# The second block's mixer laid out anew: recurrence projected first, attention scores by pairs of heads, and the feed-forward's first weight splits earlier

## The chip, the core and the metric

The kernel runs on one core of a Trainium2 chip. The metric is device time in microseconds (us). The engines are TensorE (PE in the rows; PEld is its weight load), VectorE (DVE), ScalarE (ACT), GpSimd (POOL) and SyncE (SP, which here only issues DMA transfers). A trailing q, as in SPq, stands for an engine's queue.

## What is computed

Two transformer blocks on 256 tokens of width 1024 in fp32. The first holds two attention mixers and a mixture of 32 experts, and its weights of some 400 MB fill most of the time. The change lies in the second block, which is, cut to what matters:

```python
h = rms_norm(x, g_pre_mix)
q, k, v, xr, gr = split(h @ w_in)                     # 5 chunks of 512 columns
attn = softmax(q k^T / 8 + bias, causal) @ v          # 8 heads of 64
xr = causal_dwconv(xr, w_conv_lru, b_conv_lru)        # 4 taps
r = sigmoid(xr @ w_r + b_r); i = sigmoid(xr @ w_i + b_i)   # block-diagonal
log_a = -8 * r * softplus(-lam); a = exp(log_a)
u = sqrt(-expm1(2 * log_a)) * (i * xr)
lru = scan(h_t = a_t * h_(t-1) + u_t) * gelu(gr)
x = x + rms_norm(concat([attn, lru]) @ w_out, g_post_mix)
h = rms_norm(x, g_pre_ffn)
up = causal_dwconv(h @ w_up)                          # 2 * 2816 columns, 3 taps
x = x + rms_norm((gelu(up_g) * up_u) @ w_down, g_post_ffn)
```

## The kernel before, in words

**Precision.** Each weight and each activation is split into a high part rounded to fp32r (a copy on ScalarE, tiles `wh`, `uh`, `mxh`) and a low part, the rest (a subtraction on VectorE, tiles `wl`, `ul`, `mxl`). A product is three matmuls, high by high, high by low and low by high (`mm3`, L288 to L291). `split` (L267) and `row_split` (L1280) do this for a tile of 128 x 1024 of a weight. They take their tiles from the pool `ws`, which in the second block has 5 buffers of each name (L1291).

**Order.** The code lists instructions in program order. A planner inside the framework then lays out the queue of each engine: it lets an engine take the earliest instruction of the program that it holds to be ready, by its own costs. On the chip each queue runs in the order so fixed. `tc.issue_after` adds an edge to this plan. PSUM has 8 banks in this part, 4 named `acc` (`acc_tile`) and 4 named `wk` (`work_tile`), each name a ring.

**Weights.** The list `plan` (L182 to L217) gives the order in which SyncE loads them, each into one of 3 ring buffers (`NRING_A`, L90). `done(key)` frees a buffer once its last split has read it, and that issues the next load of the list. For the second block the list is: 5 chunks of `w_in` ("in2": v, q, k, xr, gr), 2 halves of `w_out` ("o2"), then 11 chunks of `w_up` with 6 of `w_down` between them.

**The stages around the change.**

- `x2_norm` (L1408) makes the first block's final norm and the second block's first one: sums of squares on ScalarE, `rsq` and `rs_sum` with a power on GpSimd, and `spread_tile` (L338), which turns the column `r2` into a row `rB` by a matmul. `rB` scales every projected chunk when it leaves PSUM.
- The projection loop (before the line `for _ in heads`, L1600) runs 16 weight tiles of 24 matmuls, 4 a chunk in the order q, k, xr, gr (`seq`). `presplit(j + 2)` stands ahead of the matmuls of tile j. After xr come `conv` (L1455); after gr come `lru_gates` (L1461, block-diagonal matmuls and tanh) and `lru_a` (L1468, exp, tanh, square).
- From the third chunk on, two steps of the generator `attention` (L1547) follow each tile. `a_s(h)` (L1498) makes one head's scores (contraction over 64 rows) and its softmax, `a_t(h)` (L1520) transposes them, `a_o(p)` (L1529) multiplies by v for two heads. It uses an `acc` bank.
- Behind the loop `lru_b` (L1482) has square root, gelu and scan, and `mxh`/`mxl` 4 to 7 (the recurrence's half of the input of `w_out`) are split.
- `nat2` (L1310) runs `w_out`: 48 matmuls of 512 columns with the first half (rows of the attention), whose four row tiles are split ahead as `first`, then 48 with the second. `epi2` (L1648) holds the norms behind it; while the second 128 tokens go through theirs, 24 dummy matmuls run.
- `split_up(i)` (L1615) splits the feed-forward's weight tile i. Tiles 0 to 2 are split ahead of `nat2`; the low parts of 0 and 1 are made on GpSimd (`eng=G`), that of 2 on VectorE. Tile 1 borrows the buffers `xc`, `ig`, tile 2 `rg`, `vN`. Tile 3 comes behind the transposes at the end of `epi2`.

Of the kernel before, what the change touches and what calls it, by code (L numbers as in the profile page):

```python
# [25 lines left out]
FT = mybir.dt.float32  # L26
FR = mybir.dt.float32r
# [77 lines left out]
def block_kernel(ctx: ExitStack, tc: tile.TileContext, A, out, dbg=None, parts=("t1", "moe", "over", "t3")):  # L105
# [105 lines left out]
    for c in range(2):  # L211
        want(("o2", c), wo2[c], [P, 4, 1024])
# [541 lines left out]
    ts(ch, ch, -4.0, None, OP.mult)  # L754

# [652 lines left out]
    def x2_norm(t):  # L1408
        rms_halves(r1[:, t:t + 1], xn[:, t], sm)
        tt(xn[:, t], xn[:, t], gfin, OP.mult)  # L1410
        ss = sm.tile([P, 1], FT, name="ss", bufs=4)
        sumsq(ss, xn[:, t], tp.tile([P, D], FT, name="junk2"))
        ts(ss, ss, r1[:, t:t + 1], r1[:, t:t + 1], OP.mult, OP.mult)
        rsq(r2[:, t:t + 1], ss, D, sm)
        tt(r2[:, t:t + 1], r2[:, t:t + 1], r1[:, t:t + 1], OP.mult)
        ts(xn[:, t], xn[:, t], r1[:, t:t + 1], None, OP.mult)
# [51 lines left out]
    def lru_a(hf):  # L1468
# [5 lines left out]
        for m in (2 * hf, 2 * hf + 1):  # L1474
            act(a_[:, m], rg[:, m], AF.Exp, scale=ch[:, m:m + 1], bias=ch[:, m:m + 1])
            ts(rg[:, m], rg[:, m], ch[:, m:m + 1], ch[:, m:m + 1], OP.mult, OP.add)
        stt(ig[:, ms], ig[:, ms], 1.0, xc[:, ms], OP.add, OP.mult)
        act(rg[:, ms], rg[:, ms], AF.Tanh, scale=-1.0)
# [19 lines left out]
    def a_s(h):  # L1498
        z = work_tile()
        p, r0 = h // 2, 64 * (h % 2)  # L1500
        PE.matmul(z[:, 0:P], qT[r0:r0 + 64, p, 0:P], kT[r0:r0 + 64, p, 0:P], start=True, stop=False,
                  skip_group_check=True)
        PE.matmul(z[:, P:384], qT[r0:r0 + 64, p, P:S], kT[r0:r0 + 64, p, 0:S], start=False, stop=True,
                  skip_group_check=True)
        s = mx_.tile([P, 384], FT, name="as", bufs=3)
        tt(s[:, 0:P], z[:, 0:P], Bt[:, h, P:S], OP.add)
        tt(s[:, P:384], z[:, P:384], Bt[:, h], OP.add)
        nm = sm.tile([P, 2], FT, name="nm", bufs=4)
        V.reduce_max(nm[:, 0:1], s[:, 0:P], axis=AX, negate=True)
        V.reduce_max(nm[:, 1:2], s[:, P:384], axis=AX, negate=True)  # L1510
        rs = sm.tile([P, 2], FT, name="rsum", bufs=4)
        act(s[:, 0:P], s[:, 0:P], AF.Exp, bias=nm[:, 0:1], accum_out=rs[:, 0:1])
        act(s[:, P:384], s[:, P:384], AF.Exp, bias=nm[:, 1:2], accum_out=rs[:, 1:2])
        rc = sm.tile([P, 2], FT, name="rcp", bufs=4)
        V.reciprocal(rc, rs)
        ts(s[:, 0:P], s[:, 0:P], rc[:, 0:1], None, OP.mult)
        ts(s[:, P:384], s[:, P:384], rc[:, 1:2], None, OP.mult)
        pm[h] = s
# [10 lines left out]
    def a_o(p):  # L1529
        o = acc_tile()  # L1530
# [16 lines left out]
    def attention():  # L1547
        a_s(0)
        yield
        for h in range(8):  # L1550
            if h + 1 < 8:
                a_s(h + 1)
                yield
            a_t(h)
            if h % 2 == 1:
                a_o(h // 2)
            yield
# [14 lines left out]

    heads = attention()
    presplit(0)
    presplit(1)
    for j, ((i, hf, m), _) in enumerate(seq):
# [6 lines left out]
        if m == 1:  # L1583
            if i == 1:
                stt(qT[:, sl], ps, 0.125, rB2, OP.mult, OP.mult)
            elif i == 2:
                tt(kT[:, sl], ps, rB2, OP.mult)
            elif i == 3:
# [3 lines left out]
            else:  # L1592
# [70 lines left out]
    for i in range(3):  # L1663
        split_up(i)
# [186 lines left out]
```

## Time and profile before

| what | value |
|---|---|
| median of 3 runs (lowest to highest) | 1423.74 us (1421.06 to 1424.24) |
| the profiled execution, its time | 1422.5 us |
| its span, first to last instruction | 1420.5 us |
| TensorE matmul busy | 1315.2 us (93%) |
| VectorE busy | 627.6 us (44%) |
| ScalarE busy | 371.8 us (26%) |
| GpSimd busy | 40.0 us (3%) |
| mean DMA rate | 340 GB/s |

The time is the span and some 2 us around it. Busy shares are means over stages with different limits: the experts fill the middle of the span with DMA at 427 GB/s, the second block runs from about 1081 us to the end. Matmuls are pipelined, so their recorded durations overlap; what one of a stream costs is the distance between the starts of neighbours. The idle time in brackets at the end of a timeline row is that of the engine just before the row's instruction, with the engine that ended it.

### The profile page before, as it was taken

What the parts mean: (1) busy time and instruction counts of PE and PEld (TensorE: products, weight loads), DVE (VectorE), ACT (ScalarE), POOL (GpSimd) and SP (SyncE); (2) the same over time, 40 slices, a digit from 0 to 9 for tenths busy, and PEclk for the clock granted to TensorE, in tenths of its full rate; (3) what the DMA queues carried; (4) which work ended last, traced back from release to release, by engine and by line L of the source; (5) the groups of instructions that cost most, each with busy time, mean ns of one, the idle gap of its engine ahead of it and who ended that gap; (6) DMA issues with size and microseconds to landing.
All of it is one profiled execution on the core that took longest, in us unless ns stands there. A gap on an engine that the chain in (4) does not pass through costs nothing.

```text
span 1420.5 us, 19855 instructions
## 1 busy us (share of the span) xinstructions
PE 1315.2 (93%) x8393; PEld 744.0 (52%) x8394; DVE 627.6 (44%) x1250; ACT 371.8 (26%) x641; POOL 40.0 (3%) x54
## 2 busy tenths in 40 slices
PE   8989999999998888889998888988888998999997
PEld 7777543434333333333343333333335886899997
DVE  6766532332322232222232222322226878677776
ACT  5654211101100010001110001100014658555554
POOL 1010200000000000000000000000000101000000
PEclk9999999999999999999999999999999999999999
DMA  7366899999999999999999999999998523355530
GB/s 287 112 239 270 340 427 427 426 427 426 427 427 427 427 427 426 425 412 427 427 427 427 427 428 427 427 426 427 427 426 350 188 103 134 138 196 197 196 149 31
DMA packets 40591, 482.40 MB, mean 340 GB/s; under 512 B 4104, under 2 KB 4640, under 8 KB 12592
## 3 DMA queue, kind: packets, MB, share of 16 engines
q1 hardware_dynamic: 39232, 477.99, 81.2%
q0 software_dynamic: 832, 2.62, 0.6%
q8 instruction: 68, 1.11, 0.3%
q10 hardware_dynamic: 432, 0.46, 0.1%
q14 instruction: 27, 0.22, 0.0%
HBM read 479.99 MB, written 1.06 MB: 339 GB/s over the span
## 4 chain that ended last, share of the span: by engine, by line
DMA 47%; PE 45%; DVE 4%; issue 2%; ACT 2%; POOL 1%; DVEq 0%; ACTq 0%; SPq 0%; POOLq 0%
DMA w<-w_gu 25%; DMA w<-w_dn 19%; PE gu L1086 10%; PE y L1122 4%; PE acc L289 3%; PE acc L290 3%; PE acc L291 3%; PE wk L290 3%; PE wk L291 3%; PE wk L289 3%; DMA w<-w_pg 2%; PE pj L289 1%; PE pj L291 1%; PE pj L290 1%; PE xg L1056 1%
## 5 line engine op out<-in xcount | busy, mean ns | idle before, releaser
L1086 PE MATMUL gu<-w,xg 128*64 128x512 f32 x2048 | 470.1, 601 | 45.2 <-DMA w<-w_gu 39.1
L1086 PEld LDWEIGHTS gu<-w,xg 128*64 128x64 f32 x2048 | 141.6, 137 | 315.4 <-issue 249.8
L1122 PE MATMUL y<-w,gl 128*64 128x512 f32 x1024 | 233.1, 597 | 28.9 <-DMA w<-w_dn 27.2
L121 ACT ACTIVATE h<-gu,gs 128x512 f32<-128x512 f32 x64 | 40.5, 683 | 558.8 <-PE gu L1086 558.8
L124 DVE TENSOR_TENSOR h<-sc,h 128x512 f32<-128x512 f32 x126 | 81.4, 686 | 201.0 <-PE sc L1146 198.5
L273 DVE TENSOR_TENSOR wl<-w,wh 128x1024 fp32r<-128x1024 f32 (+2 forms) x124 | 147.5, 1200 | 45.5 <-ACT wh L121 45.0
L1122 PEld LDWEIGHTS y<-w,gl 128*64 128x64 f32 x1024 | 73.5, 136 | 161.3 <-issue 157.9
L121 ACT ACTIVATE wh<-w 128x1024 fp32r<-128x1024 f32 (+2 forms) x125 | 128.2, 1038 | 91.0 <-PE acc L291 21.6
L124 DVE TENSOR_TENSOR gl<-tr,bgu 128x512 f32<-128x512 f32 x32 | 22.1, 692 | 270.1 <-PE tr L1101 270.1
L290 PE MATMUL wk<-ul,wh 128*128 128x256 f32 x336 | 94.5, 281 | 0.2 <-DVE ul L124 0.2
L289 PE MATMUL wk<-uh,wh 128*128 128x256 f32 x336 | 94.5, 281 | 0.0
L291 PE MATMUL wk<-uh,wl 128*128 128x256 f32 x336 | 94.3, 281 | 0.0
L121 ACT ACTIVATE sg<-gl 128x512 f32<-128x512 f32 x32 | 20.1, 629 | 183.0 <-DVE gl L131 183.0
L290 PEld LDWEIGHTS wk<-ul,wh 128*128 128x128 f32 x336 | 63.4, 189 | 1.2 <-DVE ul L124 0.4
L1071 DVE CAST gt<-y 128x256 fp32r<-128x256 f32 x32 | 13.6, 424 | 114.0 <-PE y L1069 114.0
L289 PEld LDWEIGHTS wk<-uh,wh 128*128 128x128 f32 x336 | 63.3, 188 | 1.0 <-ACT uh L121 0.2
L291 PEld LDWEIGHTS wk<-uh,wl 128*128 128x128 f32 x336 | 63.4, 189 | 0.0
L1056 PE MATMUL xg<-oh,u 128*128 128x64 bf16 x1536 | 50.0, 193 | 0.7 <-ACT proj L121 0.7
L1056 PEld LDWEIGHTS <-u 128*128 128x128 bf16 x1536 | 49.1, 98 | 2.6 <-issue 2.3
L127 DVE SCALAR_TENSOR_TENSOR cv<-wk,vec,cv 128x255 f32<-128x255 f32 x88 | 42.3, 480 | 8.7 <-ACT cv L121 7.1
L127 DVE SCALAR_TENSOR_TENSOR sg<-y,gs,li 128x512 fp32r<-128x512 f32 x31 | 23.3, 751 | 49.7 <-ACT li L121 49.7
L121 ACT ACTIVATE li<-y,gs 128x512 fp32r<-128x512 f32 x31 | 21.3, 687 | 80.9 <-PE y L1122 79.4
(419 smaller groups left out, 1753.3 us busy)
## 6 DMA issues: line engine op xcount, KB each, us to landing
w<-w_gu SPq DMA_DIRECT2D x128, 2048.0 KB, 39.1
w<-w_dn SPq DMA_DIRECT2D x63, 2048.0 KB, 39.1
w<-w_up SPq DMA_DIRECT2D x11, 2048.0 KB, 7.8
w<-w_in SPq DMA_DIRECT2D x7, 2048.0 KB, 9.5
w<-w_down SPq DMA_DIRECT2D x5, 2048.0 KB, 7.6
w<-w_o SPq DMA_DIRECT2D x4, 2048.0 KB, 8.6
w<-w_pg SPq DMA_DIRECT2D x2, 2048.0 KB, 35.4
w<-w_in SPq DMA_DIRECT2D x2, 1024.0 KB, 8.3
```

Source lines behind the costliest of these rows:

```text
L121: return SC.activation(out=o, in_=i, func=f, **kw)
L124: return V.tensor_tensor(out=o, in0=a, in1=b, op=op)
L127: return V.scalar_tensor_tensor(out=o, in0=a, scalar=s, in1=b, op0=op0, op1=op1)
L273: eng.tensor_tensor(out=lo, in0=src, in1=hi.bitcast(FT), op=OP.subtract)
L289: PE.matmul(o, l[0], r[0], start=first, stop=False)
L290: PE.matmul(o, l[0], r[1], start=False, stop=False)
L291: PE.matmul(o, l[1], r[0], start=False, stop=last)
L1056: PE.matmul(px[:, kd], u3[i][:, t, kd * P:(kd + 1) * P], oh[:, t], start=(n == 0), stop=(n == 5))
L1071: V.tensor_copy(gt, pgt[:, 0:S])
L1086: PE.matmul(ps[64 * s:64 * s + 64, n], xg[:, k], w[:, kk, s * 1024 + n * 512:s * 1024 + (n + 1) * 512], start=(k == 0), stop=(k == 7))
L1122: i = PE.matmul(ps[64 * s:64 * s + 64], aT[:, k], w[:, kk, s * 512:(s + 1) * 512], start=(k == 0), stop=(k == 7))
```

## The change

`w_in`'s chunks come in another order, v, xr, gr and then two chunks that hold 256 columns of q and the same of k. The halves of `w_out` are loaded and used in the order 1, 0. In the projection loop the convolution belongs to chunk 1, the gates to chunk 2, and `lru_b` with the splits of `mxh` 4 to 7 stands behind the first half of chunk 3. `a_s` takes two heads; its matmuls are listed head by head within each block of queries. The generator steps once a tile in chunk 4 and once per token tile in the half of `w_out` that belongs to the recurrence; `a_o` takes a `wk` bank. `w_out`'s second part (the attention's) follows when all heads are through. The low parts of `split_up` all go to VectorE, 0 and 1 ahead of that second part's splits, 2 and 3 behind them, 3 in the buffers `gr` and `wri`. `lru_a` takes the tanh of a scaled and shifted input in one activation (new column `nch = -ch`) in place of a VectorE step and an activation; `x2_norm` folds two scalings into one `scalar_tensor_tensor`.

```diff
-    for c in range(2):
+    for c in (1, 0):
         want(("o2", c), wo2[c], [P, 4, 1024])
...
+    nch = keep.tile([P, 4], FT, name="nch")
+    ts(nch, ch, -1.0, None, OP.mult)
...
     def x2_norm(t):
         rms_halves(r1[:, t:t + 1], xn[:, t], sm)
-        tt(xn[:, t], xn[:, t], gfin, OP.mult)
+        stt(xn[:, t], xn[:, t], r1[:, t:t + 1], gfin, OP.mult, OP.mult)
         ss = sm.tile([P, 1], FT, name="ss", bufs=4)
         sumsq(ss, xn[:, t], tp.tile([P, D], FT, name="junk2"))
-        ts(ss, ss, r1[:, t:t + 1], r1[:, t:t + 1], OP.mult, OP.mult)
         rsq(r2[:, t:t + 1], ss, D, sm)
         tt(r2[:, t:t + 1], r2[:, t:t + 1], r1[:, t:t + 1], OP.mult)
-        ts(xn[:, t], xn[:, t], r1[:, t:t + 1], None, OP.mult)
         spread_tile(rB, r2, t, sm, work_tile)
...
             act(a_[:, m], rg[:, m], AF.Exp, scale=ch[:, m:m + 1], bias=ch[:, m:m + 1])
-            ts(rg[:, m], rg[:, m], ch[:, m:m + 1], ch[:, m:m + 1], OP.mult, OP.add)
+            act(rg[:, m], rg[:, m], AF.Tanh, scale=nch[:, m:m + 1], bias=nch[:, m:m + 1])
         stt(ig[:, ms], ig[:, ms], 1.0, xc[:, ms], OP.add, OP.mult)
-        act(rg[:, ms], rg[:, ms], AF.Tanh, scale=-1.0)
...
-    def a_s(h):
+    def a_s(p):
+        zs = [work_tile() for _ in range(2)]
+        for q in range(2):
+            for i in range(2):
+                r0 = 64 * i
+                o = zs[i][:, 0:P] if q == 0 else zs[i][:, P:384]
+                PE.matmul(o, qT[r0:r0 + 64, p, q * P:(q + 1) * P], kT[r0:r0 + 64, p, 0:(q + 1) * P],
+                          start=(q == 0), stop=(q == 1), skip_group_check=True)
+        for i in range(2):
+            h, z = 2 * p + i, zs[i]
+            s = mx_.tile([P, 384], FT, name="as", bufs=4)
...
     def a_o(p):
-        o = acc_tile()
+        o = work_tile()
...
-        for h in range(8):
-            if h + 1 < 8:
-                a_s(h + 1)
+        for p in range(4):
+            if p + 1 < 4:
+                a_s(p + 1)
                 yield
-            a_t(h)
-            if h % 2 == 1:
-                a_o(h // 2)
+            a_t(2 * p)
+            yield
+            a_t(2 * p + 1)
+            a_o(p)
             yield
...
+    def o2_mm(i, hl, t, n, last):
+        sl = slice(n * 512, (n + 1) * 512)
+        mm3(acc2[t][n], (mxh[:, i, t * P:(t + 1) * P], mxl[:, i, t * P:(t + 1) * P]),
+            (hl[0][:, sl], hl[1][:, sl]), i == 4, last)
...
             if i == 1:
-                stt(qT[:, sl], ps, 0.125, rB2, OP.mult, OP.mult)
-            elif i == 2:
-                tt(kT[:, sl], ps, rB2, OP.mult)
-            elif i == 3:
                 tt(xr[:, sl, 3:3 + S], ps, rB2, OP.mult)
                 conv(2 * hf)
                 conv(2 * hf + 1)
-            else:
+            elif i == 2:
                 tt(gr[:, sl], ps, rB2, OP.mult)
                 lru_gates(2 * hf)
                 lru_gates(2 * hf + 1)
                 lru_a(hf)
-        if i >= 3:
-            next(heads, None)
-            next(heads, None)
+            elif hf == 0:
+                stt(qT[:, 2 * i - 6:2 * i - 4], ps, 0.125, rB2, OP.mult, OP.mult)
+            else:
+                tt(kT[:, 2 * i - 6:2 * i - 4], ps, rB2, OP.mult)
+        if i == 3 and m == 1 and hf == 0:
+            lru_b()
+            for k in range(4):
+                act(mxh[:, 4 + k], gr[:, k])
+                tt(mxl[:, 4 + k], gr[:, k], mxh[:, 4 + k].bitcast(FT), OP.subtract)
+        if i == 4:
+            take(1)
+
+    acc2 = [[acc_tile() for _ in range(2)] for _ in range(2)]
+    first = [row_split(("o2", 1), i) for i in range(2)]
+    for i in range(4):
+        if i + 2 < 4:
+            first.append(row_split(("o2", 1), i + 2))
+        for t in range(2):
+            for n in range(2):
+                o2_mm(4 + i, first[i], t, n, False)
+            take(1)
+    done(("o2", 1))
     for _ in heads:
         pass
-    lru_b()
...
-        if i in (1, 2):
-            hi, lo = [mx_.tile([P, 8, P], FR, name=n) for n in (("xc", "ig"), ("rg", "vN"))[i - 1]]
+        if i in (1, 2, 3):
+            hi, lo = [mx_.tile([P, 8, P], FR, name=n) for n in (("xc", "ig"), ("rg", "vN"), ("gr", "wri"))[i - 1]]
             src = src_T(("up", 0), j % 2, m)
             act(hi, src)
-            (G if i < 2 else V).tensor_tensor(out=lo, in0=src, in1=hi.bitcast(FT), op=OP.subtract)
+            tt(lo, src, hi.bitcast(FT), OP.subtract)
             wup[i] = hi, lo
         else:
-            wup[i] = split(ws, src_T(("up", j // 2), j % 2, m), eng=G if i < 1 else V)
+            wup[i] = split(ws, src_T(("up", j // 2), j % 2, m))
...
-    for i in range(3):
+    for i in range(2):
         split_up(i)
-    nat2([("o2", 0), ("o2", 1)], tok(mxh, mxl), epi2, first)
+    sp = [row_split(("o2", 0), i) for i in range(4)]
+    done(("o2", 0))
+    split_up(2)
+    split_up(3)
+    for t in range(2):
+        for n in range(2):
+            for i in range(4):
+                o2_mm(i, sp[i], t, n, i == 3)
+        epi2(t, acc2[t])
...
-    with tc.issue_after(held["hi"].ins), tc.issue_after(held["turn"].ins):
-        split_up(3)
```

`take(n)` draws n steps from the generator `heads`. The host array `w_in2` is packed in the new order of chunks.

## Rows read from the trace of the kernel before

**Rows 1.** Stretches: us, busy of PE, PEld, DVE, ACT, POOL, clock, DMA share, GB/s

```profile
1128.42:1147.90 19.48, 19.48 (x164) 19.48 (x164) 12.40 (x13) 7.22 (x7) 0.00 (x0) 1.00 0.63 240
1150.95:1181.70 30.75, 30.60 (x209) 24.64 (x209) 27.97 (x78) 20.83 (x52) 0.00 (x0) 1.00 0.23 82
1188.00:1204.77 16.77, 13.93 (x61) 10.01 (x59) 12.82 (x16) 12.31 (x19) 5.35 (x2) 0.98 0.34 126
1204.77:1211.26 6.49, 6.49 (x16) 5.14 (x17) 3.67 (x4) 1.84 (x2) 0.00 (x0) 0.54 0.30 71
```

**Rows 2.** Timeline, TensorE: start, us, instruction, idle before it, releaser

```profile
1187.43 0.70 PE L1524 MATMUL wk<-cf,as 128*128 128x128 f32 x3 [1.29 <-DVE as L131]
1203.26 0.50 PE L290 MATMUL acc<-wl,uh 128*128 128x512 f32 x1 [2.06 <-DVE wl L273]
1204.77 1.22 PE L289 MATMUL acc<-wh,uh 128*128 128x512 f32 x2 [0.78 <-ACT wh L121]
1217.51 0.39 PE L290 MATMUL acc<-wl,uh 128*128 128x512 f32 x1
1217.74 0.40 PE L291 MATMUL acc<-wh,ul 128*128 128x512 f32 x1
```

**Rows 3.** Timeline, GpSimd and then VectorE, same columns, beside the idle time

```profile
1196.17 2.82 POOL L273 TENSOR_TENSOR wl<-w,wh 128x1024 fp32r<-128x1024 f32 x1 [71.10 <-ACT wh L121]
1198.94 2.58 POOL L1623 TENSOR_TENSOR ig<-w,xc 128x1024 fp32r<-128x1024 f32 x1
...
1195.16 0.42 DVE L124 TENSOR_TENSOR ul<-gr,uh 128x256 fp32r<-128x256 f32 x1
1196.68 2.58 DVE L124 TENSOR_TENSOR ul<-gr,uh 128x256 fp32r<-128x256 f32 x1
1199.19 2.88 DVE L124 TENSOR_TENSOR gr<-rg,gr 128x512 f32<-128x512 f32 x1
```

**Rows 4.** Timeline, TensorE, two neighbours in the slow stretch

```profile
1208.35 0.63 PE L289 MATMUL acc<-wh,uh 128*128 128x512 f32 x1
1208.78 0.63 PE L290 MATMUL acc<-wl,uh 128*128 128x512 f32 x1
```

**Rows 5.** Timeline, TensorE: scores of two heads, then of one

```profile
1148.13 0.50 PE L1501 MATMUL wk<-kT,qT 64*128 64x128 f32 x4
...
1149.00 0.39 PE L289 MATMUL acc<-uh,wh 128*128 128x256 f32 x1
...
1162.85 0.48 PE L1501 MATMUL wk<-kT,qT 64*128 64x128 f32 x2
...
1163.70 0.38 PE L289 MATMUL acc<-uh,wh 128*128 128x256 f32 x1
```

**Rows 6.** Timeline, ScalarE, a split; SyncE, loads of w_out; page, their landing

```profile
1139.48 1.06 ACT L121 ACTIVATE wh<-w 128x1024 fp32r<-128x1024 f32 x1 [1.82 <-PE acc L290]
...
1133.19 11.90 SPq L244 DMA_DIRECT2D w<-w_o  x2
...
w<-w_o SPq DMA_DIRECT2D x4, 2048.0 KB, 8.6
```

**Rows 7.** Groups by form, VectorE 1145 to 1190; ScalarE 1121 to 1228

```profile
L127 DVE SCALAR_TENSOR_TENSOR xc<-xr,vec,xc 128x256 f32<-128x256 f32 x12 | 5.1, 476 | 0.0
...
L121 ACT ACT_TABLE_LOAD x5 | 6.4, 1283 | 0.1
```

**Rows 8.** Timeline, VectorE: softmax of the first two heads, first and last step

```profile
1149.09 0.62 DVE L124 TENSOR_TENSOR as<-wk,w 128x128 f32<-128x128 f32 x2 [1.53 <-PE wk L1503]
...
1153.84 0.54 DVE L131 TENSOR_SCALAR as<-as,rcp 128x128 f32<-128x128 f32 x2
```

**Rows 9.** Timeline, GpSimd, VectorE and TensorE, around the second block's first norm

```profile
1119.47 1.46 POOL L311 TENSOR_TENSOR r<-rs_m,halfneg 128x1 f32<-128x1 f32 x1 [0.34 <-DVE rs_m L127]
...
1119.31 1.22 DVE L124 TENSOR_TENSOR h<-h,gfin 128x1024 f32<-128x1024 f32 x1
...
1121.91 0.38 PE L291 MATMUL acc<-uh,wl 128*128 128x256 f32 x1 [0.41 <-DVE wl L273]
```

More of the change, by code (lines that the diff above doesn't have):

```diff
@@ L1496, in block_kernel @@
     at_, pm = {}, {}
-    def a_s(h):
[L1499 to L1518, printed above, removed]
@@ new lines, in a_s @@
+    def a_s(p):
[9 more added lines that the diff above has]
+            s = mx_.tile([P, 384], FT, name="as", bufs=4)
+            tt(s[:, 0:P], z[:, 0:P], Bt[:, h, P:S], OP.add)
+            tt(s[:, P:384], z[:, P:384], Bt[:, h], OP.add)
+            nm = sm.tile([P, 2], FT, name="nm", bufs=4)
+            V.reduce_max(nm[:, 0:1], s[:, 0:P], axis=AX, negate=True)
+            V.reduce_max(nm[:, 1:2], s[:, P:384], axis=AX, negate=True)
+            rs = sm.tile([P, 2], FT, name="rsum", bufs=4)
+            act(s[:, 0:P], s[:, 0:P], AF.Exp, bias=nm[:, 0:1], accum_out=rs[:, 0:1])
+            act(s[:, P:384], s[:, P:384], AF.Exp, bias=nm[:, 1:2], accum_out=rs[:, 1:2])
+            rc = sm.tile([P, 2], FT, name="rcp", bufs=4)
+            V.reciprocal(rc, rs)
+            ts(s[:, 0:P], s[:, 0:P], rc[:, 0:1], None, OP.mult)
+            ts(s[:, P:384], s[:, P:384], rc[:, 1:2], None, OP.mult)
+            pm[h] = s
@@ L1571, in presplit, with take @@
                 done(("in2", i))
+    def o2_mm(i, hl, t, n, last):
+        sl = slice(n * 512, (n + 1) * 512)
+        mm3(acc2[t][n], (mxh[:, i, t * P:(t + 1) * P], mxl[:, i, t * P:(t + 1) * P]),
+            (hl[0][:, sl], hl[1][:, sl]), i == 4, last)
+    def take(n):
+        for _ in range(n):
+            next(heads, None)
     heads = attention()
@@ L1596, in block_kernel @@
                 lru_a(hf)
-        if i >= 3:
-            next(heads, None)
-            next(heads, None)
+            elif hf == 0:
[19 more added lines that the diff above has]
+    done(("o2", 1))
     for _ in heads:
         pass
-    lru_b()
-    for m in range(4):
-        act(mxh[:, 4 + m], gr[:, m])
-        tt(mxl[:, 4 + m], gr[:, m], mxh[:, 4 + m].bitcast(FT), OP.subtract)
     uh, ul = new_u(t3)
@@ L1609, in block_kernel @@
     SY.dma_start(gpre, row_ap(A["g_pre_ffn"], D))
-    first = [row_split(("o2", 0), i) for i in range(4)]
-    done(("o2", 0))
     wdn, wup, acts = {}, {}, {}
@@ L1795, in host_arrays @@
     q, k, v, xr, gr = (w[:, i * 512:(i + 1) * 512] for i in range(5))
-    f["w_in2"] = c(np.concatenate([rows(v), pairs(q), pairs(k), pairs(xr), pairs(gr)], axis=0))
+    qk2 = [np.stack([colchunks(q, 256)[i], colchunks(k, 256)[i]], axis=1)[None] for i in range(2)]
+    f["w_in2"] = c(np.concatenate([rows(v), pairs(xr), pairs(gr)] + qk2, axis=0))
     f["rel_bias"] = c(g["rel_bias_2"])
```

## The prediction

> **What bounds the kernel now.** I read the busy times by stretch first, then TensorE's timeline for every gap, then the timelines of the engines that ended the gaps. From 1081 us on TensorE is the bound: in the first chunks of the projection it is busy for the whole stretch, and with heads, convolution and gates beside the projection it still is, though VectorE is busy for 27.97 of 30.75 us there [rows 1]. A stage of the second block is thus worth what TensorE waits in it, or runs slowly in it. That is concentrated between the projection and the middle of `w_out`. TensorE waits 1.29 us for a head's softmax, 2.06 us for the low part of a split and 0.78 us for the high part of one [rows 2]: 4.13 us. Right behind these waits the granted clock is 0.54 over 6.49 us [rows 1], mostly the lower of its two levels (1.2 and 2.4 GHz): neighbouring matmuls of 512 columns start 0.43 us apart [rows 4], against 0.23 us once the clock is back [rows 2]. The loss is 6.49 x (1 - 0.23/0.43) = 3.0 us.
>
> The cause of the two longer waits stands on GpSimd. While it makes two low parts (2.82 and 2.58 us), a VectorE subtraction that takes 0.42 us takes 2.58 us, and the product behind it 2.88 us [rows 3]. That product closes the recurrence, and the splits of `w_out` queue behind it.
>
> **What the change removes.** (a) The 4.13 us of waits and the 3.0 us of slow clock. The recurrence would be finished some six weight tiles before `w_out` needs it. A tile takes 19.48 us x 24/164 matmuls = 2.85 us [rows 1], so that is 17 us, and `w_out` starts with the recurrence's half while the heads still run. GpSimd makes no low part any more. (b) Scores by pairs. Two heads on different halves of the array's rows, queued together, take from 1148.13 to 1149.00 = 0.87 us; one head alone takes from 1162.85 to 1163.70 = 0.85 us [rows 5]. So the second head costs 0.02 us. The kernel before has the pair once (heads 0 and 1) and six single heads: 6 x 0.85 = 5.10 us become 3 x 0.87 = 2.61 us, a gain of 2.5 us. All other matmuls stay: 16 tiles, the gates, 24 transposes, four products with v, 96 matmuls of `w_out`.
>
> **What it adds or moves, and what covers it.**
>
> The two low parts go to VectorE, where a split of this size is one instruction. It lies beside the recurrence's half of `w_out`, 48 x 0.23 = 11 us of TensorE plus the head steps between. VectorE has there two pairs' softmax, the low parts of the coming rows and these two; in the stretch of before where it had eight heads' worth of such work and the convolution it was 91% busy without a stall on TensorE [rows 1]. I cost it at nothing.
>
> The convolution now falls into the first chunk. There VectorE's own load is 12.40/19.48 = 64% [rows 1], or 7.3 us of a chunk's 11.4. Sixteen steps of the convolution at 5.1/12 = 0.43 us [rows 7] add 6.8 us, so it ends the chunk 2.7 us behind. The cover is the lead of the splits: ScalarE waits 1.82 us at every split for TensorE to free a buffer [rows 6], so with five buffers some four tiles are ready ahead, 11 us. Cost nothing; without that lead it would be the 2.7 us.
>
> Square root and gelu move between the splits of chunk 3. Each change of table takes 1.283 us on ScalarE [rows 7], three such (to the square root, to gelu, back to exp) 3.8 us. A split there needs 1.06 us in 2.85 [rows 6], so this too stays inside the lead. The one activation for two steps in `lru_a` takes a round trip to VectorE off a chain that no longer ends anything.
>
> `x2_norm`: the product with the gain ran beside GpSimd's power (start 1119.31 and 1119.47) and now waits for it; behind it on VectorE stand the splits of the first tiles, and ScalarE's sum, the copies of v and the matmul of `spread_tile` wait for it. This is not in the trace. Bounds: +1.2 us, the whole product on the path, and -0.41 us, TensorE's wait for the first low part, if the two VectorE steps that go away let it come earlier [rows 9]. Between these I take 0, as both apply; `rB` itself is first needed when a pair of tiles is through.
>
> DMA: the halves of `w_out` change places in SyncE's queue. Both were issued by 1133.19 + 11.90 = 1145.1 us and land 8.6 us later [rows 6], some 20 us before either is used. `w_up` and `w_down` move forward with the chunks that free their buffers. The load of `g_pre_ffn` waits for the last scores on SyncE and holds back one load of `w_up` behind it, which is not read before the feed-forward. Nothing.
>
> The hand-over from one half of `w_out` to the other: the last row tile of the second part takes a buffer that the first part frees with its last matmul, and `mxh` 3 comes out of the last `a_o`. TensorE has the last transposes, the product with v and nine matmuls of 0.23 us to do meanwhile. Bounds: 0, and 2.84 us, the two waits for splits at the like place of before. I take the nearer row, 0.78 us for a high part behind ScalarE's other work [rows 2], as the work that stood on VectorE is gone. `split_up(2)` waits for v's last reader; behind it on VectorE stands only `split_up(3)` and then the norm, which comes 24 matmuls later.
>
> **The sum.** Against the profiled execution (1422.5 us, of which 1420.5 span): -4.13 - 3.0 - 2.5 + 0.8 = -8.8 us, 1413.7 us. The median of the runs is 1.24 us above that execution, so 1423.74 - 8.8 = 1414.9 us. With the bounds, -10.0 to -5.6 us: 1413.7 to 1418.1; the runs of before lie up to 2.7 us below their median, so the case's own range is 1411.5 to 1418.1.
>
> **Rivals.**
>
> (1) The pairs gain nothing, since a pair leaves the same work for VectorE. For it: VectorE's first step to its last takes from 1149.09 to 1154.38 us for the first pair [rows 8], six times the matmuls. Against it: in the new layout three half-rows of `w_out`, 18 x 0.23 = 4.1 us, and head steps lie between a pair's scores and its transposes. Price: the 2.5 us, so 1417.4 us. The Trainium skill speaks for this rival: TensorEngine Tiling (Array Packing), section PSUM Bottleneck, says that packing the array speeds up TensorE but not the emptying of PSUM. By that rule alone the sum would be -6.3 us, by the scores' rows -8.8; the trace agrees that the time behind the scores is far longer than they are.
>
> (2) The wait at the hand-over is as long as before, 2.84 us, and the clock falls again, 3.0 us: -4.13 - 3.0 - 2.5 + 2.84 + 3.0 = -3.8 us, 1419.9 us. For it: the same five buffers serve both parts. Against it: TensorE now has head steps to fill with, and VectorE has no 2.58 us subtraction.
>
> (3) Slower: the splits get in front of the softmax on VectorE. The last two pairs must be through while only `w_out` is left to run. If splits hold each back by over 3.3 us, both latencies show: 2 x 5.3 us [rows 8] and one fall of the clock, 3.0 us, make +13.6 us against -9.6, so +4.0 us, 1427.7 us. It decides from 9.6 us of new waits in all. Against it: the heads stand earlier in the program than those splits, so the planner gives them VectorE first, and 91% busy did no harm [rows 1].
>
> (4) The change does not do what it says: the planner, by its own costs, still puts square root, gelu and scan behind the exps, `w_out` still waits for them as long as now and the clock falls. Only the pairs are left: 1423.74 - 2.5 = 1421.2 us.
>
> **Chances.** The forecast 0.70, rival (1) 0.08, (2) 0.12, (3) 0.05, (4) 0.05. The predicted time is the likeliest case's, 1414.9 us. From 1411.5 to 1420.0 lie the forecast, (1) and (2), about 0.88; taking (2) in is what brings it above 0.8 when the bounds of the unknown terms come out badly. A measurement of this kernel can tell about 0.2%, 2.85 us: faster means under 1420.9 us. The forecast, (1) and most of (2) are faster, 0.88; (4) and the rest of (2) are the same, 0.07; (3) is slower, 0.05.
>
> **What would show it.** Right: no TensorE wait above 1 us and a granted clock of 1.0 from the projection to the dummy matmuls; four groups of scores with four matmuls each per form, 0.87 us to the next stream; no tensor operation on GpSimd but the powers; the scan over before the last third of the projection; the end of `w_out` 9 us earlier, and the feed-forward as long as now. Wrong: waits for the softmax at the transposes (1 or 3), for a split between the two parts of `w_out` (2), for `mxh` at the start of `w_out` (4), or a later first tile of the projection (`x2_norm`). If the time moves and the stretch between projection and feed-forward has not shrunk, the cause lies elsewhere and the sum is wrong.

## The result, and the profile after

The changed kernel takes 1413.63 us (median of 3 runs, 1413.1 to 1414.68) against 1423.74 us: a ratio of 0.994, 95% interval 0.9926 to 0.9954. A second comparison in five rounds gave 1413.63 against 1421.94 us, ratio 0.9941 (0.9927 to 0.9955). The profiled execution took 1413.63 us, of which 1412.0 are span; against that of before (1422.5 and 1420.5) it is 8.87 us shorter, where the sum said 8.8; the medians differ by 10.1 us in the first comparison and by 8.3 in the second.

The first view is the table of stretches of the kernel after (us, busy time of PE, weight loads, DVE, ACT and POOL, granted clock, DMA share, GB/s): the projection from its last head-free chunk on, then both halves of `w_out` with the heads, then the norm.

```profile
1140.00:1163.90 23.90, 23.00 (x186) 22.43 (x184) 15.67 (x23) 23.75 (x37) 0.00 (x0) 1.00 0.30 115
1163.90:1176.00 12.10, 12.10 (x95) 10.51 (x95) 11.99 (x34) 9.49 (x23) 0.00 (x0) 1.00 0.47 169
1176.00:1186.00 10.00, 9.24 (x51) 6.33 (x51) 8.66 (x24) 7.42 (x17) 0.00 (x0) 1.00 0.23 69
1186.00:1199.00 13.00, 13.00 (x68) 8.59 (x68) 10.86 (x22) 8.04 (x18) 0.00 (x0) 1.00 0.39 156
1199.00:1209.00 10.00, 10.00 (x44) 7.83 (x42) 5.36 (x10) 3.43 (x11) 1.11 (x2) 1.00 0.99 385
```

The clock is granted in full in all five; the stretch at 0.54 [rows 1] has no successor. POOL has nothing to do until 1199 us. Beside the first pairs VectorE is nearly as full as TensorE (11.99 against 12.10 of 12.10 us), and TensorE waits for nothing there. TensorE's timeline from the 16 transposes that open the second block on has these waits, and no others (start, us, instruction, idle before it and who ended it; the rows without brackets are for orientation):

```profile
1082.41 1.97 PE L1390 MATMUL wk<-cf,h 128*128 128x128 f32 x16 [2.34 <-DVE h L124]
...
1111.05 0.51 PE L289 MATMUL acc<-wh,uh 128*128 128x512 f32 x1 [0.96 <-ACT uh L121]
...
1163.89 0.39 PE L291 MATMUL acc<-uh,wl 128*128 128x256 f32 x1 [0.90 <-DVE wl L273]
...
1184.10 0.80 PE L1539 MATMUL wk<-pT,vN 128*64 128x256 f32 x3 [0.76 <-ACT pT L121]
...
1208.74 0.40 PE L291 MATMUL acc<-wh,ul 128*128 128x512 f32 x1
...
1216.40 1.29 PE L1664 MATMUL wk<-cf,xr 128*128 128x128 f32 x8 [0.60 <-DVE xr L127]
...
1218.44 0.38 PE L290 MATMUL wk<-ul,wh 128*128 128x256 f32 x1 [0.22 <-DVE ul L124]
```

Where before had 1.29, 2.06 and 0.78 us [rows 2], after has 0.90 and 0.76 us. The last matmul of `w_out` starts at 1208.74, 9.00 us earlier than the 1217.74 of before [rows 2]. The scores, with the neighbour before and the two behind:

```profile
1186.07 0.40 PE L291 MATMUL acc<-wh,ul 128*128 128x512 f32 x1
1186.40 0.93 PE L1503 MATMUL wk<-kT,qT 64*128 64x128 f32 x8
1187.25 0.50 PE L289 MATMUL acc<-wh,uh 128*128 128x512 f32 x1
1187.59 0.39 PE L290 MATMUL acc<-wl,uh 128*128 128x512 f32 x1
```

Two heads take 0.85 us to the next stream, as one head did alone [rows 5]; the four groups read 0.85 or 0.86 us each. The rows show a second cost, which I had not counted: 0.33 us instead of 0.23 to get into the group and 0.34 instead of 0.23 for the first matmul behind it. A group thus costs another 0.2 us, and there are three fewer.

**Account of the 8.87 us**, along TensorE. From the end of the 16 transposes (1084.94 before, 1084.38 after) to the last matmul of `w_out` it was 132.80 us and is 124.36. In that: the old waits less the new ones, -4.13 + 0.90 + 0.76 = -2.47; the clock -3.0, as the prediction worked it out; scores -2.5; the three group changes -0.6; the stage with `x2_norm` +0.63 (VectorE begins to empty the projection's second tile at 1128.44 before and at 1128.51 after, though the block began 0.56 us earlier); the remaining -0.5 are small gaps I can't place. Behind it: the norm 0.07 longer, the feed-forward 0.41 longer. Not from the change: the experts end 0.56 us earlier and what lies around the span is 0.37 us less. Together -8.9. Without the last two the change is worth 7.9 us in this pair of profiles.

### The profile page after: what moved, and what is told of

It reads as the page before. It is cut to its first block, busy times and chain, and to the rows that moved or that the text cites. A ratio compares the mean times of both kernels' runs of the same rounds, so it can differ in the third digit from the quotient of the medians.

```text
span 1412.0 us, 19848 instructions
## 1 busy us (share of the span) xinstructions
PE 1309.4 (93%) x8393; PEld 738.1 (52%) x8394; DVE 622.0 (44%) x1245; ACT 374.2 (27%) x644; POOL 32.4 (2%) x52
## 3 DMA queue, kind: packets, MB, share of 16 engines
HBM read 479.99 MB, written 1.06 MB: 341 GB/s over the span
## 4 chain that ended last, share of the span: by engine, by line
DMA 48%; PE 41%; DVE 5%; ACT 3%; issue 2%; POOL 1%; DVEq 0%; ACTq 0%; SPq 0%; POOLq 0%
DMA w<-w_gu 28%; DMA w<-w_dn 18%; PE gu L1088 9%; PE y L1124 4%; PE wk L290 3%; PE wk L291 3%; PE wk L289 3%; PE acc L289 3%; PE acc L291 3%; PE acc L290 3%; DMA w<-w_in 2%; PE pj L289 1%; PE pj L291 1%; PE pj L290 1%; PE xg L1058 1%
## 5 line engine op out<-in xcount | busy, mean ns | idle before, releaser
L127 DVE SCALAR_TENSOR_TENSOR cv<-wk,vec,cv 128x255 f32<-128x255 f32 (+1 forms) x88 | 41.9, 480 | 10.9 <-ACT cv L121 9.5
```

The costliest lines, as they stand in the source:

```text
L127: return V.scalar_tensor_tensor(out=o, in0=a, scalar=s, in1=b, op0=op0, op1=op1)
```

## The experiments

Whole times of this kernel spread by some 3 us, so beside them I use **S**: from the end of those 16 transposes to the feed-forward's first row `wk<-ul,wh` (at 1218.44 in the fence above). It holds all that was edited. It has two parts, up to the last matmul of `w_out`, and the norm behind it. The runs were made in three groups, in which the kernel before had medians of 1422.45 (e1 to e4), 1422.94 (e5 to e8) and 1421.94 us (e10 to e13); each ratio is to the kernel before of its own group.

| kernel | median us | ratio, 95% | S | to the end of `w_out` | norm |
|---|---|---|---|---|---|
| before | 1423.74 | | 142.43 | 132.80 | 9.63 |
| after | 1413.63 | 0.994, 0.9926 to 0.9954 | 134.06 | 124.36 | 9.70 |
| e1, pairs alone | 1419.05 | 0.9978, 0.9968 to 0.9988 | 137.81 | 127.41 | 10.40 |
| e2, no GpSimd alone | 1418.7 | 0.9973, 0.9963 to 0.9982 | 137.22 | 127.43 | 9.79 |
| e10, both on before | 1419.7 | 0.9978, 0.9969 to 0.9988 | 138.82 | 124.07 | 14.75 |
| e11, new order alone | 1419.29 | 0.9981, 0.9971 to 0.9992 | 138.16 | 128.46 | 9.70 |
| e3, after, single heads | 1417.8 | 0.9969, 0.9956 to 0.9981 | 137.85 | 127.96 | 9.89 |
| e4, after, with GpSimd | 1415.67 | 0.9951, 0.9934 to 0.9967 | 134.87 | 125.17 | 9.70 |
| e5, after, old norm | 1414.41 | 0.9938, 0.9921 to 0.9955 | 133.46 | 123.76 | 9.70 |
| e6, tables together | 1414.72 | 0.9935, 0.9919 to 0.9952 | 133.99 | 124.30 | 9.69 |
| e7, splits held | 1412.62 | 0.9924, 0.9908 to 0.9941 | 133.81 | 124.11 | 9.70 |
| e8, heads written first | 1413.61 | 0.993, 0.9914 to 0.9947 | 134.24 | 124.54 | 9.70 |
| e12, e5 and e7 | 1413.32 | 0.9943, 0.9929 to 0.9956 | 134.30 | 124.60 | 9.70 |
| e13, after again | 1413.63 | 0.9941, 0.9927 to 0.9955 | 134.00 | 124.30 | 9.70 |

In e1 and e12 the granted clock was low at the start of the block, ahead of everything edited: the first matmul of `spread_tile` comes 36.94 us after the transposes in e1, 35.84 in before, and 37.20 in e12, 36.05 in e5 with the same norm. The 1.1 us are in the table; the text says where they are taken off. S comes from one execution of each kernel. In the medians e1, e2, e10 and e11 gain 1.2 to 1.6 us less than in S, so how often the clock falls in `w_out` in the other executions is not known. My theory was that of the prediction: the waits and the clock fall come from work on VectorE and GpSimd, and the pairs are worth their TensorE time. Its rivals are named with each run.

### Two parts of the change alone, and together

**e1: the kernel before, with `a_s(p)` and `attention()` of after**, and so also with four buffers of the softmax's tile `as` where before has three.

> The kernel before with nothing changed but the scores by pairs of heads. Theory of the sum: three more pairs at 0.87 us in place of six single heads at 0.85 us each, so -2.5 us, about 1421.2 us where before is 1423.7. Rival 1 (the pairs only move the waiting to the softmax): 0 us, and TensorE waits some 2.5 us longer at the transposes (line of a_t).

```diff
-    def a_s(h):
+    def a_s(p):
...
-        for h in range(8):
-            if h + 1 < 8:
-                a_s(h + 1)
+        for p in range(4):
+            if p + 1 < 4:
+                a_s(p + 1)
                 yield
-            a_t(h)
-            if h % 2 == 1:
-                a_o(h // 2)
+            a_t(2 * p)
+            yield
+            a_t(2 * p + 1)
+            a_o(p)
```

1419.05 against 1422.45 us, -3.4; S is 4.6 us less, 5.7 without the low clock at its start. More than the 2.5 us of the scores. Its stretches of `w_out`, and TensorE's timeline with the waits there:

```profile
1188.00:1204.00 16.00, 14.97 (x64) 11.35 (x62) 10.73 (x15) 13.85 (x20) 5.70 (x2) 1.00 0.37 132
1204.00:1212.00 8.00, 7.24 (x30) 5.66 (x31) 6.92 (x11) 3.96 (x10) 0.57 (x1) 1.00 0.51 170
```

```profile
1201.32 0.50 PE L290 MATMUL acc<-wl,uh 128*128 128x512 f32 x1 [0.23 <-DVE wl L273]
1204.57 0.50 PE L289 MATMUL acc<-wh,uh 128*128 128x512 f32 x1 [1.37 <-ACT uh L121]
1205.26 0.50 PE L290 MATMUL acc<-wl,uh 128*128 128x512 f32 x1 [0.18 <-DVE wl L273]
```

GpSimd still works for 5.70 us there and the recurrence is still late, but its waits are shorter than those of [rows 2] and the clock stays at 1.00. So the pairs remove the fall of the clock too, without touching GpSimd. That the shorter waits are the reason, and what part the fourth buffer has in it, was not tried by itself.

**e2: the kernel before, all low parts on VectorE.**

> The kernel before with nothing changed but the two low parts of split_up, made on VectorE. Theory that GpSimd's two instructions are the cause of the waits of 2.06 and 0.78 us and of the slow clock behind them: -5.8 us (1417.9 us), no wait over 1 us in w_out, granted clock 1.0 there, the 1.29 us wait for a softmax stays. Rival, the layout is the cause (the recurrence ends last whatever GpSimd does): 0 to -2 us, and the clock still falls in w_out.

```diff
-            (G if i < 2 else V).tensor_tensor(out=lo, in0=src, in1=hi.bitcast(FT), op=OP.subtract)
+            tt(lo, src, hi.bitcast(FT), OP.subtract)
...
-            wup[i] = split(ws, src_T(("up", j // 2), j % 2, m), eng=G if i < 1 else V)
+            wup[i] = split(ws, src_T(("up", j // 2), j % 2, m))
```

S is 5.2 us less; 5.8 were expected. In its trace the 2.06 and 0.78 us are gone, 1.06 us for a low part is left in their place (none over 1 us was expected), the wait for the softmax stays as it was and the clock is full:

```profile
1189.43 0.70 PE L1524 MATMUL wk<-cf,as 128*128 128x128 f32 x3 [1.28 <-DVE as L131]
...
1204.94 0.50 PE L290 MATMUL acc<-wl,uh 128*128 128x512 f32 x1 [1.06 <-DVE wl L273]
```

So in the old order GpSimd's two subtractions caused the long waits, as read from [rows 3], and without them the clock holds.

**e10: both edits on the kernel before.** The question was whether the new order adds anything to them.

> The kernel before with the pairs of heads and with VectorE's low parts, in the old order of chunks and halves. From the end of the first 16 transposes of the second block to the feed-forward's first matmuls the kernel before takes 142.4 us, the pairs alone 137.8, no GpSimd alone 137.2, the changed kernel 134.1. Theory that the three parts add up and both single edits already take the fall of the clock away (3.0 us counted twice): -4.6 - 5.2 + 3.0 = -6.8, 135.6 us, and the new layout is worth the last 1.5 us. Rival, the layout is worth nothing once these two are there: 134.1 us, as the changed kernel.

S is 138.82 us, above either edit alone; both expectations fell. The part up to the end of `w_out`, though, is 124.07 us, as short as in the changed kernel. What is lost is lost behind it, where the norm takes 14.75 us. TensorE's timeline there, with ScalarE's first sum of squares of token tile 0 below it, and the stretch:

```profile
1210.28 0.40 PE L291 MATMUL acc<-wh,ul 128*128 128x512 f32 x1
1214.02 1.97 PE L1647 MATMUL wk<-cf,qT 128*128 128x128 f32 x8 [3.35 <-DVE qT L127]
1215.64 7.53 PE L1662 MATMUL wk<-uh 128*128 128x512 f32 x24
...
1207.96 0.60 ACT L121 ACTIVATE junk<-acc 128x512 f32<-128x512 f32 x1 [4.47 <-PE acc L291]
```

```profile
1212.00:1224.00 12.00, 9.98 (x40) 8.32 (x40) 7.03 (x13) 4.44 (x13) 1.64 (x3) 0.72 0.13 57
```

The planner mixed the matmuls of the two token tiles: in the program 36 matmuls stand behind the twelve that the first sum waits for, and here some ten are left when it starts. So the first tile's sums begin only 2.3 us before the last matmul, and its norm isn't covered: TensorE waits 3.35 us, and the 24 dummy matmuls that keep it busy take 7.53 us in a stretch whose clock is 0.72. In the changed kernel's timeline the sum and the dummies stand like this:

```profile
1200.77 0.60 ACT L121 ACTIVATE junk<-acc 128x512 f32<-128x512 f32 x1 [1.68 <-PE acc L291]
...
1210.10 5.70 PE L1679 MATMUL wk<-uh 128*128 128x512 f32 x24
```

There the sums begin 8.0 us before the last matmul, since only the second half of `w_out` is left and it runs tile by tile; no wait, and 5.70 us for the dummies. The kernel before had 5.8 us (1211.99 to 1217.74). Up to the end of `w_out`, then, the new order adds next to nothing to the other two edits; what it adds beside them, 4.8 us of S, is the covered norm.

**e11: the new order alone**, the changed kernel with single heads and GpSimd's low parts (the edits of e3 and e4, below). The small edits (`x2_norm`, `lru_a`, `a_o`'s bank, the fourth buffer of `as`) stay in it.

> The changed kernel with single heads and with GpSimd's low parts, so the new layout without the other two edits. Theory that the parts stand for themselves there: 134.1 + 3.8 + 0.8 = 138.7 us of the stretch that is 142.4 before, the clock at 1.0. Rival, the layout needs the other two: waits of 2 us and more come back, the clock falls, 141 us or more.

S is 138.16 us, 4.3 less than before, at a full clock; 138.7 were expected if the parts stand for themselves there. So each of the three parts alone brings 4.3 to 5.7 us, and all of them 8.4: by the rows each contains the 3.0 us of the clock, which can be won only once, and part of the same waits.

### Parts taken out of the changed kernel

**e3: single heads.**

> The changed kernel with the heads' scores one at a time again, in 16 steps. Theory of the sum: eight single heads at 0.85 us in place of four pairs at 0.86 us, +3.4 us, 1417.0 us where the changed kernel has 1413.6. Rival 1 (pairs gain nothing, the softmax sets the pace): within 0.5 us of the changed kernel.

```diff
-    def a_s(p):
+    def a_s(h):
...
-        for p in range(4):
-            if p + 1 < 4:
-                a_s(p + 1)
+        for h in range(8):
+            if h + 1 < 8:
+                a_s(h + 1)
                 yield
-            a_t(2 * p)
-            yield
-            a_t(2 * p + 1)
-            a_o(p)
+            a_t(h)
+            if h % 2 == 1:
+                a_o(h // 2)
...
-            take(1)
+            take(2 - t)
```

3.8 us more in S, and some 4 us by the ratios (0.9969 against 0.9941). Four more groups at 0.85 + 0.2 us are 4.2; the 0.76 us wait of after doesn't occur here. TensorE's timeline of one of its groups:

```profile
1189.04 0.48 PE L1500 MATMUL wk<-kT,qT 64*128 64x128 f32 x2
1189.37 0.59 PE L1502 MATMUL wk<-kT,qT 64*128 64x256 f32 x2
1189.89 0.50 PE L289 MATMUL acc<-wh,uh 128*128 128x512 f32 x1
```

One head takes 0.85 us, as the two above. The pairs are worth their full TensorE time, and rival (1) falls: VectorE has the same work in both, and its latency was covered in both.

**e4: GpSimd's low parts again.**

> The changed kernel with the low parts of the feed-forward's weight tiles 0 and 1 on GpSimd again. If GpSimd holds VectorE up as in the kernel before, two VectorE instructions take over 2.5 us each beside the softmax of the later heads: TensorE waits for the transposes or for a low part, +1 to +4 us, more if the granted clock falls. If the new layout has the slack to hide it: 0 to +0.7 us, though the long VectorE instructions are there.

```diff
-            tt(lo, src, hi.bitcast(FT), OP.subtract)
+            (G if i < 2 else V).tensor_tensor(out=lo, in0=src, in1=hi.bitcast(FT), op=OP.subtract)
...
-            wup[i] = split(ws, src_T(("up", j // 2), j % 2, m))
+            wup[i] = split(ws, src_T(("up", j // 2), j % 2, m), eng=G if i < 1 else V)
```

S is 0.8 us more, between the two expectations, nearer the slack; with single heads it is 0.3 us (e11 against e3). GpSimd's timeline and VectorE's beside it:

```profile
1183.34 2.40 POOL L1644 TENSOR_TENSOR ig<-w,xc 128x1024 fp32r<-128x1024 f32 x1 [55.53 <-DVE nm L1512]
1185.71 3.35 POOL L273 TENSOR_TENSOR wl<-w,wh 128x1024 fp32r<-128x1024 f32 x1
...
1184.27 2.55 DVE L273 TENSOR_TENSOR wl<-w,wh 128x1024 fp32r<-128x1024 f32 x1
1186.74 0.21 DVE L1517 RECIPROCAL rcp<-rsum 128x2 f32<-128x2 f32 x2
1186.93 2.93 DVE L131 TENSOR_SCALAR as<-as,rcp 128x128 f32<-128x128 f32 x4
1189.78 1.21 DVE L273 TENSOR_TENSOR wl<-w,wh 128x1024 fp32r<-128x1024 f32 x1
```

VectorE is held up as in [rows 3]: a low part takes 2.55 us beside GpSimd and 1.21 behind it, and four products of the softmax 2.93 where two take 0.54 us [rows 8]. The Trainium skill, SBUF — State Buffer, section Who interferes with whom, says that VectorE and GpSimd share a pair of ports, and that of two instructions that both need it the second stands until the first is through; these rows agree, since the low part that starts at 1184.27 ends at 1186.82, 1.08 us behind GpSimd's first one. Removing the collision from the old order gained 5.2 us, with the clock fall behind it (e2); putting it into the new one costs 0.8. Two things differ there: GpSimd no longer holds up the recurrence, which is done, and TensorE has matmuls of `w_out` to run meanwhile. No run separates the two.

**e5: the old `x2_norm`.**

> The changed kernel with x2_norm as before (product, two scalings). Theory: the folded product waits for GpSimd's power and puts ScalarE's sum of squares ahead of a copy that TensorE needs, which costs the 0.96 us wait in the v projection, of which 0.7 us is left at the end of the second weight tile; so -0.7 us (about 1412.9 where the changed kernel has 1413.6) and no such wait. Rival: the two small waits of the kernel before (0.41 and 0.18 us) come back and it is the same within 0.3 us.

```diff
-        stt(xn[:, t], xn[:, t], r1[:, t:t + 1], gfin, OP.mult, OP.mult)
+        tt(xn[:, t], xn[:, t], gfin, OP.mult)
         ss = sm.tile([P, 1], FT, name="ss", bufs=4)
         sumsq(ss, xn[:, t], tp.tile([P, D], FT, name="junk2"))
+        ts(ss, ss, r1[:, t:t + 1], r1[:, t:t + 1], OP.mult, OP.mult)
         rsq(r2[:, t:t + 1], ss, D, sm)
         tt(r2[:, t:t + 1], r2[:, t:t + 1], r1[:, t:t + 1], OP.mult)
+        ts(xn[:, t], xn[:, t], r1[:, t:t + 1], None, OP.mult)
```

S is 0.6 us less, 0.7 were expected. The 0.96 us wait at 1111.05 is gone and the 0.41 of [rows 9] is back, here at 1122.02. ScalarE's timeline of the changed kernel shows whose wait that was:

```profile
1109.59 1.06 ACT L121 ACTIVATE junk<-h 128x1024 f32<-128x1024 f32 x1
...
1110.63 0.37 ACT L121 ACTIVATE uh<-wk,gc 128x128 fp32r<-128x128 f32 x1
```

This is the norm's own sum of squares of the first token tile. It reads the product with the gain, which now waits for GpSimd's power: VectorE starts it at 1105.28 after 0.66 us of idling. In the kernel before the sum ran at 1106.12, ahead of two splits; now three splits are ahead of it (from 1105.87), and it stands for 1.06 us in front of the copy that TensorE waits for.

### The two waits that were left

**e6: gelu ahead of both square roots**, to get rid of the 0.90 us. ScalarE's timeline in the changed kernel shows four of its table loads and the work beside them:

```profile
1146.87 1.06 ACT L121 ACTIVATE wh<-w 128x1024 fp32r<-128x1024 f32 x1
1147.94 1.28 ACT L121 ACT_TABLE_LOAD   x1
1149.23 0.63 ACT L121 ACTIVATE xc<-xc 128x512 f32<-128x512 f32 x1
1149.88 1.28 ACT L121 ACT_TABLE_LOAD   x1
...
1155.24 1.28 ACT L121 ACT_TABLE_LOAD   x1
1156.53 1.06 ACT L121 ACTIVATE gr<-gr 128x1024 f32<-128x1024 f32 x1
1157.61 1.28 ACT L121 ACT_TABLE_LOAD   x1
1158.90 0.63 ACT L121 ACTIVATE xc<-xc 128x512 f32<-128x512 f32 x1
1159.44 0.71 ACT L121 ACTIVATE uh<-gr 128x256 fp32r<-128x256 f32 x2
1160.06 2.94 ACT L121 ACTIVATE wh<-w 128x1024 fp32r<-128x1024 f32 x3
```

With those at 1141.34 and 1165.52 there are six, where before had five [rows 7]: the planner puts the square root of one half of the rows before the other half's gates. Between the splits at 1146.87 and at 1160.06 ScalarE makes none, the lead of four tiles is used up, and the wait of 0.90 us follows. ScalarE is not alone in it. The high part of 1160.06 takes some 1 us, but VectorE's timeline has the end of the recurrence ahead of the low part:

```profile
1160.52 1.27 DVE L1491 TENSOR_TENSOR_SCAN rg<-xr,ig 128x256 f32<-128x256 f32 x2
...
1162.01 0.69 DVE L124 TENSOR_TENSOR gr<-rg,gr 128x512 f32<-128x512 f32 x1
1162.62 1.22 DVE L273 TENSOR_TENSOR wl<-w,wh 128x1024 fp32r<-128x1024 f32 x1
```

> The changed kernel with gelu and both square roots held behind the gates, so that ScalarE loads its table 4 times in the second mixer and not 6. Theory: the two loads (2 x 1.28 us) are what empties the lead of the splits; TensorE's wait of 0.90 us for a low part in the projection goes, -0.9 us. Rival: the wait stays, since the splits are held by something else, or it comes back at the scores: 0 us.

```diff
-        act(xc[:, ms], a_[:, ms], AF.Square)
+        held["sq"] = act(xc[:, ms], a_[:, ms], AF.Square)
...
-        for hf in range(2):
-            ms = slice(2 * hf, 2 * hf + 2)
-            act(xc[:, ms], xc[:, ms], AF.Sqrt, scale=0.25)
-        act(gr, gr, AF.Gelu_apprx_tanh)
+        with tc.issue_after(held["sq"].ins):
+            held["gelu"] = act(gr, gr, AF.Gelu_apprx_tanh)
+        with tc.issue_after(held["gelu"].ins):
+            for hf in range(2):
+                ms = slice(2 * hf, 2 * hf + 2)
+                act(xc[:, ms], xc[:, ms], AF.Sqrt, scale=0.25)
```

Four table loads, and nothing gained: S is 0.07 us less. The 0.90 us is gone, and in its place TensorE's timeline has

```profile
1166.15 0.93 PE L1505 MATMUL wk<-kT,qT 64*128 64x128 f32 x8 [1.36 <-DVE kT L124]
...
1179.29 0.43 PE L1541 MATMUL wk<-pT,vN 128*64 128x256 f32 x1 [0.53 <-ACT pT L121]
```

The first scores now wait 1.36 us for `kT`. The theory that two loads fewer are worth 0.9 us falls. In VectorE's timeline of e6 the product that makes `kT` starts at 1165.40, behind the recurrence's last product and four low parts of its output, without a pause from 1163.46 on. So here too the end of the recurrence on VectorE stands ahead of what TensorE waits for; moving it was not tried.

**e7: the feed-forward's splits behind the exps.** The 0.76 us at 1184.10 has this ahead of it in ScalarE's timeline of the changed kernel:

```profile
1178.96 1.06 ACT L121 ACTIVATE wh<-w 128x1024 fp32r<-128x1024 f32 x1 [1.53 <-DMA w<-w_up]
1179.92 1.05 ACT L121 ACTIVATE xc<-w 128x1024 fp32r<-128x1024 f32 x1
1180.88 1.05 ACT L121 ACTIVATE rg<-w 128x1024 fp32r<-128x1024 f32 x1
1181.83 0.39 ACT L121 ACTIVATE as<-as,nm 128x128 f32<-128x128 f32 x1
```

A load of `w_up` lands, three splits for the feed-forward start at once, the exps of the third pair stand behind them, and behind the exps, at 1183.58, the copies `pT` of the second pair, for which TensorE waits.

> The changed kernel with the feed-forward's splits held behind the exps of the third and the fourth pair of heads. Theory: three copies of 1 us that stand ahead of a softmax on ScalarE cause TensorE's wait of 0.76 us before the product with v; it goes, -0.8 us. Rival: the splits of the second part of w_out get late in their place and TensorE waits between the two parts: 0 to +3 us.

```diff
-            act(s[:, P:384], s[:, P:384], AF.Exp, bias=nm[:, 1:2], accum_out=rs[:, 1:2])
+            held["exp", h] = act(s[:, P:384], s[:, P:384], AF.Exp, bias=nm[:, 1:2], accum_out=rs[:, 1:2])
...
-    for i in range(2):
-        split_up(i)
+    with tc.issue_after(held["exp", 5].ins):
+        for i in range(2):
+            split_up(i)
...
-    split_up(2)
-    split_up(3)
+    with tc.issue_after(held["exp", 7].ins):
+        split_up(2)
+        split_up(3)
```

The wait is gone, but S is only 0.25 us less, of 0.8 expected; 0.5 us went into gaps too small for me to name.

**e8: all head steps written before `w_out`.**

> The changed kernel with all heads drained ahead of w_out in the program; nothing else moves. Theory: the 48 matmuls of the recurrence's half are what covers the softmax of the last two pairs, and the planner fills the gaps only as far as its costs see them: +1 to +3 us if it still draws w_out's matmuls into the gaps, +8 us and a fall of the clock if it doesn't. Rival, the heads don't need that cover: within 0.5 us.

```diff
+    for _ in heads:
+        pass
     acc2 = [[acc_tile() for _ in range(2)] for _ in range(2)]
...
-            take(1)
```

S is 0.2 us more. That the steps are written out between the row tiles of `w_out` is not what covers the heads, and that theory (1 to 3 us) falls: the planner pulls the matmuls into the gaps from wherever they stand. In its trace they still lie between the head steps. That what counts is the recurrence being done, so that they are free to run, fits this but was not tried by itself.

**e12: e5 and e7 together; e13: the changed kernel again**, five rounds of each.

> The changed kernel with the old x2_norm and the feed-forward's splits held behind the exps. If their gains in the stretch add up (0.60 and 0.25 us): 133.2 us of it where the changed kernel has 134.1, and 0.8 us less in all, which five rounds can just not tell from the changed kernel. If the second only moves a wait: 133.5 us.

> The changed kernel itself, beside the others of this call. Ratio to the kernel before 0.994 as in its first measurement, 134.1 us in the stretch.

Without the low clock at its start S of e12 is 134.30 - 1.15 = 133.15 us, as expected, 0.85 less than in e13. In the whole time that doesn't show: ratios 0.9943 (0.9929 to 0.9956) and 0.9941 (0.9927 to 0.9955). No kernel here is faster than the changed one beyond the measurement.

## Why the prediction was right, and where it was off

The time forecast was 1414.9 us, measured 1413.63; the profiled difference was forecast at 8.8 us and is 8.87, of which 0.9 us doesn't come from the change. The steps:

- **Waits and clock, right.** The three waits and the stretch at 0.54 are gone, by the cause read from [rows 3]: e2 removes it alone and gains 5.2 us of S, with the program's order as it was. What the step left out is that pairs (e1) or the order (e11) do away with the clock fall too, and that the early recurrence is enough (e11) but not needed: with the other two edits the old order reaches the end of `w_out` as early (124.07 us in e10, 124.36 after). The terms were right for the whole change, but couldn't have been handed to its parts. The recurrence's lead was overrated: 17 us were reckoned, and from the end of its last low part at 1165.10 to the first matmul of `w_out` at 1175.71 it is 10.6, which was enough.
- **Pairs, right.** 0.85 us for two heads; 2.5 us forecast, 3.8 us measured for eight singles against four pairs (e3), 3.4 us by the same arithmetic. The entry and exit of a stream, 0.2 us a group, was missing from the price.
- **The hand-over, too high.** Costed at 0.8 us, it is 0: TensorE has no wait between the halves of `w_out`. The lower of its two bounds was the right one.
- **`x2_norm`, too low.** Taken at 0, it is +0.63 in the traces and 0.6 in e5, inside its bounds of -0.41 to +1.2. The prediction named ScalarE's sum among what waits for the later product, and that is the path; but it weighed only the delay itself, not that the sum would come behind three splits and in front of a copy for TensorE. The 0.41 us [rows 9] that it set against this is gone too, but TensorE comes there later by the 0.96 us, so what removed it isn't shown.
- **Square root and gelu, wrong in size.** I counted three loads inside the lead of four tiles. There are six, five of them up to the second square root, 6.4 us at 1.283 us, with the gates and the gelu beside them, and ScalarE is busy for 23.75 of 23.90 us. The lead didn't hold, and 0.90 us is left. I had taken the program's order for the planner's, and had left out that VectorE's end of the recurrence falls into the same microseconds; with four loads (e6) the wait only moves to `kT`.
- **Low parts on VectorE, convolution, DMA: nothing, as costed.** TensorE has no wait from 1111.05 to 1163.89, where the convolution lies. From there to the norm, where the low parts lie, it has only the 0.76 us, which e7 puts on ScalarE's splits.
- **Rival (3)'s mechanism is there, in small, on ScalarE instead of VectorE:** splits in front of the exps and of `pT`, 0.76 us instead of two waits of 5.3. **(1)** falls by e3 (the Trainium skill's rule that stood beside it, TensorEngine Tiling (Array Packing), section PSUM Bottleneck, does not bite here: the pairs are worth 3.8 us), **(2)** by the missing wait at the hand-over, **(4)** by VectorE's last scans, from 1160.52 on, before the first scores at 1164.68.
- **The feed-forward** was forecast as long as before and is 0.41 us longer. All kernels built on the changed one have this, and those built on the old one don't. Its cause is open.

By size: +0.90 and +0.76 of new waits and +0.63 + 0.41 weren't in the sum; against them stand the 0.8 us for the hand-over, 0.6 us for streams, 0.5 us not placed and 0.9 us not from the change. The errors were some 3 us on either side, and that they cancel to 0.1 is chance; a gain in the forecast's range, 5.6 to 10.0 us, is not.

## What to carry to other kernels

A wait has a price only together with what the waiting engine could run instead: GpSimd's collision with VectorE cost 5.2 us where it held up the recurrence and TensorE had nothing else, and 0.3 to 0.8 us where the recurrence was done and half a product was free to run. Terms of a sum that rest on the same fall of the clock are won once, by whichever edit comes first, so parts measured alone may not be added. And where a planner sets the order, read its order from the trace, not from the program: twice here (the table loads, the sum of squares) what cost time was where the planner put an instruction, and once (e10) two good edits together uncovered the norm behind them.

## What the runs showed of the hardware

- **Waits and the granted clock.** Granted 0.54 over 6.49 us behind waits of 2.06 and 0.78 us close together [rows 1, 2], 0.72 over 12 us around a wait of 3.35 (e10), but 1.00 with waits of 1.28 and 1.06 us far apart (e2), or 1.37 with two under 0.25 beside it (e1). The length of a wait alone doesn't decide it, as the last point shows.
- **Beside GpSimd, VectorE's products with a column are held too**, not only operations on two tensors: 2.93 us for four in e4.
- **A power on GpSimd of 128 x 1 elements** takes 0.54 to 0.56 us alone (four rows of the changed kernel from 1204.54 on), and up to 1.53 us while VectorE works beside it (1118.43); before had 1.46 [rows 9], and 1.47 at 1105.02, where after has 0.55 at 1104.69 beside an idle VectorE. A product that waits for such a step waits longer where VectorE is busy.
- **At the start of the second block** all 14 traces have the same wait of 2.33 or 2.34 us before the 16 transposes. From 1082 to 1086 us the granted clock was 1.00 in seven of them and 0.57 to 0.76 in the other seven (e1, e2, e4, e6, e7, e8 and e12), with nothing edited before that. Transposes and the way to `spread_tile` together are 1.3 to 1.6 us longer in those seven; most of it lies ahead of S, except in e1 and e12.
